# The second norm of an adaLN block: squares written where the normed rows go, and modulated rows of three blocks kept in the place of the decays

## The chip, the cores and the metric

The kernel runs on one core of a Trainium2 chip. The core has a matrix engine (PE; its weight loads are shown apart as PEld), two elementwise engines (DVE, the vector engine, and ACT, the scalar engine), a third one called POOL, and SP, which issues most DMAs. Each engine works through its own list of instructions in order; an instruction waits until the semaphores it names are reached, and everything behind it on that engine waits with it. The metric is the device time of one execution in microseconds (us).

## The reference, cut to what matters

The input is 512 tokens of 1024 numbers. A first norm, attention and a gated linear attention (GLA) give a mixed row per token, which is projected and added to the input; then comes the second norm with its modulation, and a mixer over 16,384 experts (PEER) which finds, per token and head, the best keys:

```python
mixed = jnp.concatenate([att, go], axis=-1) @ w_out[l]
x = x + gate1 * mixed

h2 = rms_norm(x, norm2_w[l]) * (1.0 + scale2) + shift2
x = x + gate2 * peer_ffn(h2, peer_wq[l], peer_subkeys[l], peer_u[l], peer_v[l])
...
q = (h @ wq).reshape(B, S, PEER_HEADS, 2, PEER_QDIM // 2)
sub_scores = jnp.einsum('bshpk,hpnk->bshpn', q, subkeys).astype(jnp.float32)
top_v, top_i = lax.top_k(sub_scores, PEER_TOPK)
...
ub = jnp.take(u, eb, axis=0)
hid = jax.nn.gelu(jnp.einsum('tkd,td->tk', ub, xb), approximate=False) * gb
vb = jnp.take(v, eb, axis=0)
return jnp.einsum('tk,tkd->td', hid, vb)
```

## The kernel before, in words

The tokens are four blocks of 128. The order of the program is: first norm, projections, attention and GLA (about the first 240 us); the output projection (`mixers`, L624) for blocks 0 and 1, then for 2 and 3; the second norm of each block (`second_norm`, L649); the queries of eight heads (`wq_head`, L733), whose scores and top-16 go to DVE; then the gate phase, in which weights of the experts are built for blocks 0 to 2 and products with the first expert table (`u_part`) are done ahead; then the products with the second table. Block 3 is done by gathering the rows of its chosen experts instead (L884, L894).

Every fp32 product is done as three matmuls on a high and a low part (`mm3`, L63 to L66). `hilo` (L55) makes the parts: ACT copies the source to the high part (L59), DVE subtracts (L60).

The second norm of one block n is a chain. ACT squares the row block x1 and sums it along the row (L232, in `norm_stats`), in a tile of the tag `h2_32` that nobody reads; `rstd_of` (L71 to L81) makes the factor in four small DVE and two small ACT instructions; DVE multiplies (L653, the normed rows `xn2`); PE transposes eight squares of 128x128 (L662, `x2t`); DVE and ACT take turns to modulate them into `h32` (L666, L669); ACT rounds the whole block to `h2Th` (L671) and DVE subtracts to get `h2Tl` (L672). For block 3 PE also transposes the modulated rows back (L678), and ACT copies them to `h2n` (L679).

Two pools of one buffer tie blocks together. `xn2` has one buffer (L650). The tag `h2_32` has one buffer too, and both the squares and the modulated rows of a block are in it: the squares of block n+1 (L232) can't be written before `h2Tl` of block n has been read out of it (L672).

`wq_head` for heads 0 and 1 works in halves of 256 tokens: `pq00` and `pq01` (bank tag `ph`) take blocks 0 and 1, are copied to `qha` by ACT (L748), and take blocks 2 and 3. Then come the scores `pss` (L754), from `qha` and the keys `skT`, which SP loads into a part of `scm` (L737).

The order of the work: a scheduler orders the instructions of each engine when the program is built, by its own model of times; only in the gate phase are the orders of DVE and POOL those of the code. Tiles of the pools `frG`, `frT` and `frA` lie on the right side of the on-chip memory. `Eg` (L142, in `frG`) holds the decays of GLA and later its gates; its last use is L545. After the norms, a pool `rt` is opened in the bytes that these pools leave: in it are `qha`, `scm`, and the index tables `iot` (L950) and `ioc` (L953).

Of the kernel before, what the change touches and what calls it, by code (L numbers as in the profile page):

```python
# [7 lines left out]
F32 = mybir.dt.float32  # L8
# [4 lines left out]
AF = mybir.ActivationFunctionType  # L13
# [4 lines left out]
P = 128  # L18
D = 1024
KD = 8  # L20
# [6 lines left out]
NL = 7  # L27
# [14 lines left out]
def peer_block_kernel(ctx: ExitStack, tc: tile.TileContext, a: dict, out: bass.AP):  # L42
    nc = tc.nc
# [27 lines left out]
    def rstd_of(pool, ss, n, w, name):  # L71
        m = pool.tile([P, w], F32, name=name + "m", tag="rsm", bufs=2)
        y = pool.tile([P, w], F32, name=name + "y", tag="rsy", bufs=2)
        t = pool.tile([P, w], F32, name=name + "t", tag="rst", bufs=2)
        nc.vector.tensor_scalar(m, ss, 1.0 / n, EPS, op0=OP.mult, op1=OP.add)
        nc.scalar.activation(y, m, AF.Ln)
        nc.scalar.activation(y, y, AF.Exp, scale=-0.5)
        nc.vector.tensor_tensor(t, y, y, OP.mult)  # L78
        nc.vector.tensor_tensor(t, t, m, OP.mult)
        nc.vector.tensor_scalar(t, t, -0.5, 1.5, op0=OP.mult, op1=OP.add)  # L80
        nc.vector.tensor_tensor(y, y, t, OP.mult)  # L81
        return y
# [34 lines left out]
    def bank(name, tag="m"):  # L117
        return banks["pool"].tile([P, 512], F32, tag=tag, bufs=BUFS[tag], name=name)

    def bank2(name):  # L120
        return psf.tile([P, 2, 512], F32, tag="sc2", bufs=1, name=name)
# [5 lines left out]
    frG = frG_s.enter_context(tc.tile_pool(name="frG", bufs=1, side="right"))  # L127
# [11 lines left out]
            lst.append(frG.tile([P, 2, 2, P], F32, tag="blk", bufs=6, name=f"{nm}{i}"))  # L139
    gv = [frG.tile([P, 512], F32, tag="gv", bufs=NT, name=f"gv{n}") for n in range(NT)]  # L140

    Eg = frG.tile([P, NL + 2, 512], F32, name="Eg")  # L142
    gg = [Eg[:, n, :] for n in range(NT)]
    mixA = [frG.tile([P, 4, P], F32, tag="mixA", bufs=NT + 1, name=f"mixA{n}") for n in range(NT)]
    xn = list(zip(gv, gg))
# [56 lines left out]
    def mod_part(v, pool, tag, bufs, pb=None, dst=None):  # L202
# [18 lines left out]
        else:  # L221
# [3 lines left out]
            nc.vector.tensor_tensor(modT[:, v * 8:v * 8 + 8], pb[:, 0:8], badaT[:, v * 8:v * 8 + 8], OP.add)  # L225
            if v == 4:
                nc.vector.scalar_tensor_tensor(aT[:, 1, :], modT[:, v * 8:v * 8 + 8], 1.0, n2T, op0=OP.add, op1=OP.mult)

    def norm_stats(src, n, pool, tag, bufs, name):
        sq = pool.tile([P, D], F32, tag=tag, bufs=bufs, name=f"sq{name}{n}")  # L230
        ss = pool.tile([P, 1], F32, tag="ss", bufs=2, name=f"ss{name}{n}")
        nc.scalar.activation(sq, src, AF.Square, accum_out=ss)  # L232
        return rstd_of(pool, ss, float(D), 1, f"r{name}{n}")

    for n in range(NT):
        sq = frA.tile([P, D], F32, tag="m4", bufs=2, name=f"sqa{n}")
        ss = frA.tile([P, 2], F32, tag="ss", bufs=2, name=f"ssa{n}")
# [3 lines left out]
        r = rstd_of(frA, ss[:, 0:1], float(D), 1, f"ra{n}")  # L241
# [50 lines left out]
    for half in range(2):  # L292
# [8 lines left out]
        for k in range(4 * half, 4 * half + 4):  # L301
            h32 = frA.tile([P, T], F32, tag="h32", bufs=4, name=f"h32_{k}")
# [311 lines left out]
    frW = frW_s.enter_context(tc.tile_pool(name="frW", bufs=1, side="right", reuse_waits="tile"))  # L614
# [9 lines left out]
    def mixers(n0):  # L624
        pair = (n0, n0 + 1)
        x1s = []
        for n in pair:
            x1s.append(frW.tile([P, D], F32, tag="x1", bufs=4, name=f"x1_{n}"))
            nc.sync.dma_start(x1s[-1], a["x"][n * P:(n + 1) * P, :])
        for q in range(2):  # L630
            qs = slice(q * 512, (q + 1) * 512)
            pw = [bank(f"pw{n}{q}") for n in pair]
            for k4 in range(0, KD, 4):
                wo = raw([P, 4, 512], f"wo{n0}{q}{k4}")
                nc.sync.dma_start(wo, a["w_out"][:, k4:k4 + 4, qs])
                for j in range(0, 4, 2):
                    oh, ol = hilo(wo[:, j:j + 2, :], [P, 2, 512], f"wo{n0}{q}{k4}{j}", nc.vector)
                    for k in (k4 + j, k4 + j + 1):
                        for i, n in enumerate(pair):
                            mm3(pw[i], mixd[n][0][k], mixd[n][1][k], oh[:, k % 2, :], ol[:, k % 2, :], k == 0,  # L640
                                k == KD - 1)
            for i, n in enumerate(pair):
                mg = frW.tile([P, 512], F32, tag="mg", bufs=2, name=f"mg{n}{q}")
                nc.vector.tensor_tensor(mg, pw[i], gate1b[:, qs], OP.mult)
                nc.vector.tensor_tensor(x1s[i][:, qs], x1s[i][:, qs], mg, OP.add)
        for i, n in enumerate(pair):
            second_norm(n, x1s[i])

    def second_norm(n, x1):  # L649
        xn2 = frW.tile([P, D], F32, tag="xn2", bufs=1, name=f"xn2_{n}")  # L650
        nc.sync.dma_start(x1d[n], x1)
        r = norm_stats(x1, n, frW, "h2_32", 1, "b")
        nc.vector.tensor_scalar(xn2, x1, r, None, op0=OP.mult)  # L653
        h32 = frW.tile([P, KD, P], F32, tag="h2_32", bufs=1, name=f"h2_{n}")
        for half in range(2):
            if half == 0 and n % 2 == 0:
                second_norm.two = bank2(f"x2t{n}")
            pt = second_norm.two[:, half] if n % 2 == 0 else bank(f"x2t{n}{half}", ("pt", "po")[half])
            pt = pt.rearrange("p (a b) -> p a b", a=4)
            for i in range(4):  # L660
                k = 4 * half + i
                nc.tensor.transpose(pt[:, i, :], xn2[:, k * P:(k + 1) * P], ident)  # L662
            for i in range(4):
                k = 4 * half + i
                if i % 2:
                    nc.vector.tensor_scalar(h32[:, k, :], pt[:, i, :], aT[:, 1, k:k + 1], modT[:, 24 + k:25 + k],  # L666
                                            op0=OP.mult, op1=OP.add)
                else:
                    nc.scalar.activation(h32[:, k, :], pt[:, i, :], AF.Identity, bias=modT[:, 24 + k:25 + k],  # L669
                                         scale=aT[:, 1, k:k + 1])  # L670
        nc.scalar.activation(h2Th[:, :, n * P:(n + 1) * P], h32, AF.Copy)  # L671
        nc.vector.tensor_tensor(h2Tl[:, :, n * P:(n + 1) * P], h32, h2Th[:, :, n * P:(n + 1) * P], OP.subtract)  # L672
        if n == GB:
            two = bank2("h2n")
            for half in range(2):
                pb = two[:, half]
                for i in range(4):
                    nc.tensor.transpose(pb[:, i * P:(i + 1) * P], h32[:, 4 * half + i, :], ident)  # L678
                nc.scalar.activation(h2n[:, half * 512:(half + 1) * 512], pb, AF.Copy)  # L679
# [465 lines left out]
```

## Time and profile before

| what | us |
|---|---|
| median of three runs | 1573.27 (1570.92 to 1573.38) |
| the profiled execution's own time | 1578.01 |
| its span, first to last instruction | 1576.2 |
| PE busy in the span | 1499.6 (95%) |
| DVE busy | 1254.0 (80%) |
| ACT busy | 689.2 (44%) |
| POOL busy | 410.0 (26%) |
| mean granted TensorE clock | 0.982 |

The profiled execution took 4.74 us more than the median. A busy PE means that a matmul is in flight, not that the array runs at full speed: the clock that was granted is shown apart, where 1.00 is 2.4 GHz and 0.50 is 1.2 GHz. Overlapping matmuls of one engine are each shown with their full duration, so the pace of a row of them is the distance of two starts. In a row of the timeline the bracket gives how long the engine had been idle before the instruction and what ended that. Line numbers are those of the kernel before; the names have lost their numbers, so that `h`, `x2t` or `xn` stand for every block's.

### The profile page before, as it was taken

To read this page: it belongs to the slowest core of one execution; us is meant where nothing else is said; L and a number is where in the kernel's file an instruction comes from. 1 tells how busy PE (TensorE), PEld (TensorE's weight loads), DVE (VectorE), ACT (ScalarE), POOL (GpSimd) and SP (SyncE) were. 2 spreads that over 40 slices of the span, in tenths; PEclk is the share of its full clock that TensorE was granted. 3 is DMA by queue.
4 is the path that set the end of the run, shared out by engine and by line. 5 is a ranking of instruction groups with operands and counts; after the bars stand their busy time and mean duration, and the time that the engine had idled before them with its cause. 6 is when DMAs were issued, how large, how long until landed. Compare 5 with 4: busy or idle time off the path is not lost.

```text
span 1576.2 us, 24415 instructions
## 1 busy us (share of the span) xinstructions
PE 1499.6 (95%) x9379; PEld 1333.6 (85%) x9379; DVE 1254.0 (80%) x2476; ACT 689.2 (44%) x1078; POOL 410.0 (26%) x327
## 2 busy tenths in 40 slices
PE   4998989599999999999899999999999999999997
PEld 3787877598998999899888888888888888888885
DVE  7578567479998988997488788878888888887987
ACT  5545475343354667565233333333333333333343
POOL 1000000044410000004143344343443444334550
PEclk9999899699999999999999999999999999999998
DMA  9254435144344867679988898989998998898893
GB/s 348 84 201 147 150 102 192 60 166 171 129 145 141 266 190 232 203 228 357 400 322 328 329 360 317 350 326 354 345 325 339 340 363 325 325 350 325 294 343 124
DMA packets 154932, 409.67 MB, mean 260 GB/s; under 512 B 10288, under 2 KB 77120, under 8 KB 142400
## 3 DMA queue, kind: packets, MB, share of 16 engines
q1 hardware_dynamic: 108736, 261.30, 46.7%
q0 software_dynamic: 36864, 134.23, 23.0%
q10 hardware_dynamic: 9216, 12.59, 2.2%
q8 instruction: 73, 1.20, 0.3%
q14 instruction: 43, 0.35, 0.1%
HBM read 366.14 MB, written 41.94 MB: 259 GB/s over the span
## 4 chain that ended last, share of the span: by engine, by line
PE 63%; DVE 2%; DMA 2%; ACT 1%; issue 0%; DVEq 0%; ACTq 0%; SPq 0%
PE acc L65 11%; PE acc L64 11%; PE acc L66 11%; PE ph L66 9%; PE ph L64 9%; PE ph L65 9%; PE pg L871 4%; DMA Gd<-gs 1%; DMA gr<-Gd 1%; DVE o L864 0%; ACT gs L873 0%; DVE o L859 0%; DVE oh L816 0%; DVE oh L819 0%; ACT ge L696 0%
## 5 line engine op out<-in xcount | busy, mean ns | idle before, releaser
L884 POOL DMA_INDIRECT gu<-in_u_dram,ix_u x128 | 169.1, 1321 | 531.4 <-DVE o L864 268.3
L894 POOL DMA_INDIRECT gv<-in_vP_dram,ix_v x128 | 168.9, 1320 | 217.8 <-DVE gu L886 187.0
L899 DVE SCALAR_TENSOR_TENSOR gacc<-gv,hg,gacc 128x1024 f32<-128x1024 f32 x127 | 162.6, 1280 | 1.7 <-DMA gv<-in_vP_dram,ix_v 1.5
L886 DVE SCALAR_TENSOR_TENSOR gu<-gu,h2n 128x1024 f32<-128x1024 f32 x128 | 155.9, 1218 | 6.2 <-DMA gu<-in_u_dram,ix_u 6.2
L1025 ACT ACTIVATE Ah<-ge 128x384 fp32r<-128x384 f32 x64 | 33.6, 525 | 157.2 <-PE acc L65 154.5
L1025 ACT ACTIVATE Ah<-gel 128x384 fp32r<-128x384 f32 x64 | 33.6, 525 | 154.4 <-PE acc L65 154.4
L873 ACT ACTIVATE gs<-pg 128x512 f32<-128x512 f32 x96 | 94.0, 1110 | 8.1 <-PE pg L871 8.0
L864 DVE TENSOR_TENSOR o<-o,gp 128x1024 bf16<-128x1024 bf16 x144 | 91.0, 687 | 4.3
L871 PE MATMUL pg<-o,o 128*128 128x128 bf16 x1152 | 77.7, 222 | 4.9 <-DVE o L864 4.9
L871 PEld LDWEIGHTS <-o 128*128 128x128 bf16 x1152 | 68.7, 98 | 13.3 <-issue 7.8
L696 ACT ACTIVATE ge<-ph 128x384 f32<-128x384 f32 x128 | 60.7, 475 | 26.3 <-PE ph L66 26.3
L1026 DVE TENSOR_TENSOR Al<-gel,Ah 128x384 fp32r<-128x384 f32 x64 | 35.5, 555 | 45.2 <-ACT Ah L1025 45.2
L950 POOL IOTA iot<- 128x256 bf16 x1 | 1.5, 1542 | 249.8 <-DVE rb0t L78 249.8
L859 DVE TENSOR_TENSOR o<-iot,t 128x2048 bf16<-128x2048 bf16 x48 | 58.5, 1218 | 4.9 <-ACT t L839 4.9
L1026 DVE TENSOR_TENSOR Al<-ge,Ah 128x384 fp32r<-128x384 f32 x64 | 35.5, 554 | 19.0 <-ACT Ah L1025 16.2
L1021 DVE TENSOR_TENSOR ge<-ge,gr 128x384 f32<-128x384 f32 x64 | 35.4, 552 | 13.3 <-ACT ge L696 13.3
L212 DVE SCALAR_TENSOR_TENSOR macc<-wa,scs,macc 128x1024 f32<-128x1024 f32 x28 | 38.9, 1390 | 5.0 <-DMA wa<-in_w_ada_dram 4.7
L1021 DVE TENSOR_TENSOR gel<-gel,gr 128x384 f32<-128x384 f32 x64 | 32.7, 552 | 0.3 <-DMA gel<-gsp 0.3
L64 PE MATMUL pq<-h2Th,wq_0h 128*128 128x512 f32 (+1 forms) x80 | 29.3, 371 | 3.0 <-ACT h2Th L671 3.0
L65 PE MATMUL pq<-h2Tl,wq_0h 128*128 128x512 f32 (+1 forms) x80 | 29.4, 367 | 0.5 <-DVE h2Tl L672 0.5
L66 PE MATMUL pq<-h2Th,wq_0l 128*128 128x512 f32 (+1 forms) x80 | 28.9, 362 | 0.0
L65 PE MATMUL pq<-h2Tl,wq_1h 128*128 128x512 f32 (+1 forms) x80 | 28.3, 354 | 0.0
(2599 smaller groups left out, 5096.3 us busy)
## 6 DMA issues: line engine op xcount, KB each, us to landing
u<-in_uT_dram SPq DMA_DIRECT2D x64, 1024.0 KB
v<-in_vP_dram SPq DMA_DIRECT2D x64, 1024.0 KB
Gd<-gs SPq DMA_DIRECT2D x24, 1024.0 KB
gr<-Gd SPq DMA_DIRECT2D x16, 1536.0 KB
wa<-in_w_ada_dram SPq DMA_DIRECT2D x20, 1024.0 KB
gsp<-ge ACTq DMA_DIRECT2D x64, 192.0 KB
gel<-gsp SPq DMA_DIRECT2D x32, 384.0 KB
wi<-in_w_in_dram SPq DMA_DIRECT2D x9, 1024.0 KB
```

Source lines behind the costliest of these rows:

```text
L64: nc.tensor.matmul(acc, lh, rh, start=start, stop=False)
L65: nc.tensor.matmul(acc, lh, rl, start=False, stop=False)
L66: nc.tensor.matmul(acc, ll, rh, start=False, stop=stop)
L864: nc.vector.tensor_tensor(o2[:, :, m], o12[:, :, 1], gp3[:, g0:g0 + H, m, None].to_broadcast([P, H, P, 2]), OP.mult)
L871: nc.tensor.matmul(pt[:, i, :], o12[:, g, 0, :, r], o2[:, g, m, :, r], start=(m == 0), stop=(m == 2))
L873: nc.scalar.activation(gs[:, :, t0 + 4 * f:t0 + 4 * f + 4].rearrange("p b a -> p a b"), pt, AF.Copy)
L884: nc.gpsimd.indirect_dma_start(out=ur, out_offset=None, in_=a["u"], in_offset=bass.IndirectOffsetOnAxis(ap=ix_u[:, s:s + 1], axis=0))
L886: nc.vector.scalar_tensor_tensor(ur, ur, 1.0, h2n, op0=OP.mult, op1=OP.mult, accum_out=hid[:, s:s + 1])
L894: nc.gpsimd.indirect_dma_start(out=vr, out_offset=None, in_=a["vP"], in_offset=bass.IndirectOffsetOnAxis(ap=ix_v[:, s:s + 1], axis=0))
L899: nc.vector.scalar_tensor_tensor(gacc, vr, hg[:, s:s + 1], gacc, op0=OP.mult, op1=OP.add)
L1021: nc.vector.tensor_tensor(ge, ge, v_part.g[:, :, c % CG, :], OP.mult)
L1026: nc.vector.tensor_tensor(Al, gef, Ah, OP.subtract)
```

## The change

`norm_stats` is gone. The squares are written into the block's own `xn2` tile, which the normed rows overwrite afterwards; `xn2` gets two buffers in place of one. The modulated rows no longer share a tag with the squares: those of block 0 have a tile of their own (`h2_0`), those of blocks 1 to 3 are three slices of one tile `h2_123`, which takes the place of `Eg` (same tag, one buffer). It can be written once L545 has read the last gate from `Eg`. The number of instructions is the same on every engine. In the new program, the lines from L236 to L647 stand 6 earlier and those from L658 on 3 later; the square is L648 and the store of x1 L646.

```diff
--- before.py
+++ after.py
@@ -139,7 +139,7 @@
             lst.append(frG.tile([P, 2, 2, P], F32, tag="blk", bufs=6, name=f"{nm}{i}"))
     gv = [frG.tile([P, 512], F32, tag="gv", bufs=NT, name=f"gv{n}") for n in range(NT)]
 
-    Eg = frG.tile([P, NL + 2, 512], F32, name="Eg")
+    Eg = frG.tile([P, NL + 2, 512], F32, tag="Eg", bufs=1, name="Eg")
     gg = [Eg[:, n, :] for n in range(NT)]
     mixA = [frG.tile([P, 4, P], F32, tag="mixA", bufs=NT + 1, name=f"mixA{n}") for n in range(NT)]
     xn = list(zip(gv, gg))
@@ -225,12 +225,6 @@
             nc.vector.tensor_tensor(modT[:, v * 8:v * 8 + 8], pb[:, 0:8], badaT[:, v * 8:v * 8 + 8], OP.add)
             if v == 4:
                 nc.vector.scalar_tensor_tensor(aT[:, 1, :], modT[:, v * 8:v * 8 + 8], 1.0, n2T, op0=OP.add, op1=OP.mult)
-
-    def norm_stats(src, n, pool, tag, bufs, name):
-        sq = pool.tile([P, D], F32, tag=tag, bufs=bufs, name=f"sq{name}{n}")
-        ss = pool.tile([P, 1], F32, tag="ss", bufs=2, name=f"ss{name}{n}")
-        nc.scalar.activation(sq, src, AF.Square, accum_out=ss)
-        return rstd_of(pool, ss, float(D), 1, f"r{name}{n}")
 
     for n in range(NT):
         sq = frA.tile([P, D], F32, tag="m4", bufs=2, name=f"sqa{n}")
@@ -647,11 +641,20 @@
             second_norm(n, x1s[i])
 
     def second_norm(n, x1):
-        xn2 = frW.tile([P, D], F32, tag="xn2", bufs=1, name=f"xn2_{n}")
+
+        xn2 = frW.tile([P, D], F32, tag="xn2", bufs=2, name=f"xn2_{n}")
         nc.sync.dma_start(x1d[n], x1)
-        r = norm_stats(x1, n, frW, "h2_32", 1, "b")
+        ss = frW.tile([P, 1], F32, tag="ss", bufs=2, name=f"ssb{n}")
+        nc.scalar.activation(xn2, x1, AF.Square, accum_out=ss)
+        r = rstd_of(frW, ss, float(D), 1, f"rb{n}")
         nc.vector.tensor_scalar(xn2, x1, r, None, op0=OP.mult)
-        h32 = frW.tile([P, KD, P], F32, tag="h2_32", bufs=1, name=f"h2_{n}")
+        if n == 0:
+            h32 = frW.tile([P, KD, P], F32, name="h2_0")
+        else:
+
+            if n == 1:
+                second_norm.h32 = frG.tile([P, NL + 2, 512], F32, tag="Eg", bufs=1, name="h2_123")
+            h32 = second_norm.h32[:, 2 * n - 2:2 * n, :].rearrange("p a (b c) -> p (a b) c", c=P)
         for half in range(2):
             if half == 0 and n % 2 == 0:
                 second_norm.two = bank2(f"x2t{n}")
```

The scheduler moves instructions. On PE, at the end of the mixers (`pw` are their products, `x2t10` and `x2t11` the transposes of block 1, `pq00` the first query product of blocks 0 and 1), before:

```order
L65 MATMUL pw31_2805<-wo2142l_2859,gh3_2487 128x512
L66 MATMUL pw31_2805<-wo2142h_2858,gl3_2488 128x512
L662 MATMUL x2t10_2704<-ident_73,xn2_1_2687 128x128 x4
L662 MATMUL x2t11_2713<-ident_73,xn2_1_2687 128x128 x4
L64 MATMUL pq00_2991<-h2Th_2428,wq0_0h_2982 128x256
L64 MATMUL pq01_2992<-h2Th_2428,wq0_0h_2982 128x256
```

and in the changed kernel:

```order
L66 MATMUL pw21_2802<-wo2142h_2856,gl2_2475 128x512
L64 MATMUL pw31_2803<-wo2142h_2856,gh3_2487 128x512
L65 MATMUL pw31_2803<-wo2142l_2857,gh3_2487 128x512
L66 MATMUL pw31_2803<-wo2142h_2856,gl3_2488 128x512
L64 MATMUL pq00_2985<-h2Th_2428,wq0_0h_2976 128x256
L64 MATMUL pq01_2986<-h2Th_2428,wq0_0h_2976 128x256
```

The eight transposes of block 1 have left this place; they stand some 60 rows further up, among the mixers' matmuls and beside the transposes of block 0, and the query products follow the mixers at once.

On ACT, at the same place in the program (`sqb` are squares, `rb` the factor, `h2_1` the modulated rows of block 1, `wq1_0h` and `uc0h` high parts of weights), before:

```order
L59 ACTIVATE uc0h_3146<-u0_3144 128x1024
L232 ACTIVATE sqb1_2689,ssb1_2690<-x1_1_2497 128x1024
L59 ACTIVATE wq1_0h_3180<-wq1_3178 128x1024
L76 ACTIVATE rb1y_2693<-rb1m_2692 128x1
L77 ACTIVATE rb1y_2693<-rb1y_2693 128x1
L669 ACTIVATE h2_1_2703<-x2t10_2704,modT_83,aT_85 128x128
L669 ACTIVATE h2_1_2703<-x2t11_2713,modT_83,aT_85 128x128
L669 ACTIVATE h2_1_2703<-x2t10_2704,modT_83,aT_85 128x128
L669 ACTIVATE h2_1_2703<-x2t11_2713,modT_83,aT_85 128x128
L671 ACTIVATE h2Th_2428<-h2_1_2703 128x8x128
L232 ACTIVATE sqb2_2882,ssb2_2883<-x1_2_2724 128x1024
```

and in the changed kernel:

```order
L672 ACTIVATE h2_0_2666<-x2t0_2667,modT_83,aT_85 128x128
L59 ACTIVATE uc0h_3140<-u0_3138 128x1024
L674 ACTIVATE h2Th_2428<-h2_0_2666 128x8x128
L59 ACTIVATE wq1_0h_3174<-wq1_3172 128x1024
L648 ACTIVATE xn2_2_2878,ssb2_2880<-x1_2_2722 128x1024
L648 ACTIVATE xn2_3_2912,ssb3_2914<-x1_3_2724 128x1024
L76 ACTIVATE rb2y_2883<-rb2m_2882 128x1
L77 ACTIVATE rb2y_2883<-rb2y_2883 128x1
L76 ACTIVATE rb3y_2917<-rb3m_2916 128x1
L77 ACTIVATE rb3y_2917<-rb3y_2917 128x1
L672 ACTIVATE h2_123_2701<-x2t2_2893,modT_83,aT_85 128x128
```

Block 1's modulation has left this place for the middle of the mixers. The squares of blocks 2 and 3 now stand back to back, and behind them the modulations of both, in turns.

On ACT, at the end of the norms (`h2n` is the copy of block 3's rows, `qha` the queries), before:

```order
L669 ACTIVATE h2_3_2932<-x2t31_2942,modT_83,aT_85 128x128
L679 ACTIVATE h2n_2430<-h2n_2953 128x512
L671 ACTIVATE h2Th_2428<-h2_3_2932 128x8x128
L679 ACTIVATE h2n_2430<-h2n_2953 128x512
L748 ACTIVATE qha_2978<-pq00_2991 128x256
L59 ACTIVATE wq1_1h_3184<-wq1_3178 128x1024
L59 ACTIVATE uc2h_3342<-u0_3144 128x1024
L748 ACTIVATE qha_2978<-pq01_2992 128x256
```

and in the changed kernel:

```order
L672 ACTIVATE h2_123_2701<-x2t2_2893,modT_83,aT_85 128x128
L674 ACTIVATE h2Th_2428<-h2_123_2701 128x8x128
L672 ACTIVATE h2_123_2701<-x2t2_2893,modT_83,aT_85 128x128
L674 ACTIVATE h2Th_2428<-h2_123_2701 128x8x128
L682 ACTIVATE h2n_2430<-h2n_2947 128x512 x2
L751 ACTIVATE qha_2972<-pq00_2985 128x256
L751 ACTIVATE qha_2972<-pq01_2986 128x256
L751 ACTIVATE qha_2972<-pq00_2985 128x256
L59 ACTIVATE wq1_1h_3178<-wq1_3172 128x1024
```

Before, the first halves of `qha` were copied between the modulations of block 2, further up. Now they stand behind `h2n`. The first of them also has a new wait: `rt` reuses the bytes of `h2_123`, so `qha` can't be written before the last `h2Tl` has read that tile. The index tables of L950 and L953 wait for it too, and so do the two `skT` loads, which stand on SP behind two stores of x1 that they preceded before. On PE the second half of `pq00` waits for the copy of its first half.

Further down the lists agree except at eight places in the gate phase, where PE does two matmuls of a next u block (`ph42`, `ph44`, `ph46`, `ph50`, `ph62`, `ph64`), a group of gate matmuls (`pg`) or one transpose earlier; ACT has a copy or a table load moved by a few rows there, and SP two stores.

## Rows read from the trace of the kernel before

**Rows 1.** One page, parts 1 and 4: busy time by engine; the chain's shares
```profile
PE 1499.6 (95%) x9379; PEld 1333.6 (85%) x9379; DVE 1254.0 (80%) x2476; ACT 689.2 (44%) x1078; POOL 410.0 (26%) x327
...
PE 63%; DVE 2%; DMA 2%; ACT 1%; issue 0%; DVEq 0%; ACTq 0%; SPq 0%
```

**Rows 2.** Busy time by stretch, us; then PEclk, DMA share, GB/s
```profile
260.00:280.00 20.00, 15.40 (x69) 11.72 (x66) 15.40 (x23) 10.74 (x16) 0.00 (x0) 1.00 0.48 166
280.00:300.00 20.00, 10.99 (x64) 9.86 (x64) 7.84 (x21) 7.99 (x16) 0.00 (x0) 0.68 0.15 57
300.00:320.00 20.00, 15.65 (x101) 14.73 (x102) 6.18 (x13) 8.48 (x16) 0.48 (x1) 0.72 0.00 1
320.00:450.00 130.00, 130.00 (x731) 118.41 (x730) 118.72 (x780) 47.17 (x67) 61.96 (x46) 1.00 0.44 155
```

**Rows 3.** Waits of PE, 250 to 320 us: total us, times, longest
```profile
PE x2t L662 <- DVE xn L653: 13.1, 2, 7.7
PE pq L64 <- ACT h2Th L671: 3.0, 1, 3.0
```

**Rows 4.** Timeline of ACT: start, us, instruction, [idle before <-releaser]
```profile
285.29 1.06 ACT L671 ACTIVATE h2Th<-h 128x1024 fp32r<-128x1024 f32 x1 [0.48 <-DVE h L666]
287.63 1.06 ACT L232 ACTIVATE sqb<-x 128x1024 f32<-128x1024 f32 x1 [1.29 <-DVE h2Tl L672]
```

**Rows 5.** Timeline of DVE, the tail of the second norm
```profile
272.95 1.22 DVE L672 TENSOR_TENSOR h2Tl<-h,h2Th 128x1024 fp32r<-128x1024 f32 x1
...
279.42 0.69 DVE L645 TENSOR_TENSOR x<-x,mg 128x512 f32<-128x512 f32 x1
...
290.24 0.76 DVE L653 TENSOR_SCALAR xn<-x,rb2y 128x1024 f32<-128x1024 f32 x1
```

**Rows 6.** Timeline of PE, from the mixers' last matmul to the scores
```profile
275.60 0.40 PE L66 MATMUL pw<-wo2142h,gl 128*128 128x512 f32 x1
281.40 1.97 PE L662 MATMUL x2t<-ident,xn 128*128 128x128 f32 x8 [5.40 <-DVE xn L653]
286.39 0.79 PE L64 MATMUL pq<-h2Th,wq_0h 128*128 128x256 f32 x2 [3.02 <-ACT h2Th L671]
...
288.25 0.41 PE L64 MATMUL pq<-h2Th,wq_0h 128*128 128x256 f32 x1
288.46 0.41 PE L65 MATMUL pq<-h2Tl,wq_0h 128*128 128x256 f32 x1
...
291.16 0.28 PE L64 MATMUL pq<-h2Th,wq_1h 128*128 128x256 f32 x1
291.28 0.28 PE L65 MATMUL pq<-h2Tl,wq_1h 128*128 128x256 f32 x1
...
318.30 1.05 PE L754 MATMUL pss<-scm,qha 128*128 128x128 f32 x8
```

**Rows 7.** Busy time by microsecond, with the granted clock (PEclk)
```profile
280.00:281.00 1.00, 0.00 (x0) 0.00 (x0) 0.90 (x5) 0.00 (x0) 0.00 (x0) 0.77 0.96 367
281.00:282.00 1.00, 0.60 (x3) 0.60 (x4) 0.34 (x1) 0.00 (x0) 0.00 (x0) 0.50 1.01 406
...
291.00:292.00 1.00, 1.00 (x11) 1.00 (x10) 0.00 (x0) 0.00 (x0) 0.00 (x0) 1.00 0.00 0
```

**Rows 8.** Groups of instructions, 276 to 318.3 us: busy, mean ns, idle before
```profile
L669 ACT ACTIVATE h<-x2t,modT,aT 128x128 f32<-128x128 f32 x12 | 5.3, 456 | 11.9 <-PE x2t L662 10.7 <-DVE h L666 1.0
...
L666 DVE TENSOR_SCALAR h<-x2t,aT,modT 128x128 f32<-128x128 f32 x12 | 4.8, 410 | 10.3 <-ACT h L669 10.3
```

**Rows 9.** Waits of PE after 320 us
```profile
PE ph L64 <- ACT ge L696: 6.3, 4, 3.6
PE pg L871 <- DVE o L864: 4.9, 8, 1.7
```

**Rows 10.** One weight tile of the gate phase: duration ns, first and last start
```profile
L64 PE MATMUL ph<-h2Th,uc42h x8: 334/334/423, 509.2 to 512.9; 128*128 128x384 f32 x8
...
L59 ACT ACTIVATE uc42h<-u x1: 1062/1062/1062, 483.8 to 483.8; 128x1024 fp32r<-128x1024 f32 x1
```

## The prediction

> **What bounds the kernel now.** I read the page's shares first, then busy time by stretch, then the waits of the engine that the first two point to, and last the timelines of the place where it waits. PE is busy in 95% of the span and holds 63% of the chain that ended last, with no other engine above 2% [rows 1]. So a microsecond in which PE stands still for another engine's work is worth about a microsecond at the end, as long as PE isn't held again later for the same reason. The stretches show where it stands still: of 260 to 320 us it is busy in 15.40, 10.99 and 15.65 us out of 20 each, and there the clock falls to 0.68 and 0.72; from 320 to 450 us it is busy all the time at 1.00 [rows 2]. DMA carries nearly nothing in 280 to 320 us (a share of 0.15 and 0.00), so no transfer is behind it.
>
> The waits name it: 13.1 us in two places for the normed rows `xn`, the longer 7.7 us, and 3.0 us for `h2Th` [rows 3]. That is the second norm's chain, and ACT's timeline shows why blocks don't overlap: the square of block 2 began 1.29 us after ACT was free, released by the subtraction that makes `h2Tl` [rows 4], because squares and modulated rows share one buffer. x1 of block 2 was long there: the last x1 row of the mixers ended at 279.42 + 0.69 = 280.1 us [rows 5], and that square began at 287.63.
>
> The price of the stretch is read on PE. The mixers' last matmul ends at 275.60 + 0.40 = 276.0 us, and the scores `pss` begin at 318.30 [rows 6]: 42.3 us. In them PE has 120 query matmuls of 256 columns (by the code, 96 of head 0 in two halves and 24 of head 1) and 32 transposes (three blocks, and the `h2n` ones). The pace of the query matmuls is 288.46 - 288.25 = 0.21 us at half clock and 291.28 - 291.16 = 0.12 us at full clock [rows 6]. Eight transposes took 1.97 us at half clock [rows 6], so about 1.0 at full clock (an estimate by the ratio of the levels). All of it at full clock and without a wait is 14.4 + 4.0 = 18.4 us, so that no reordering of this stretch alone can bring more than 42.3 - 18.4 = 23.9 us; and since block 1's eight transposes leave it, 24.9.
>
> **The change part by part.** Counts of instructions don't change; what changes is what may start when.
>
> *Block 1 into the mixers.* Its square goes to its own tile and needs `h2Tl` of block 0 no more, so its chain runs beside block 0's. It brings into 256 to 276 us one square and one `h2Th` (1.06 each [rows 4]), four modulations on ACT (4 x 0.456) and four on DVE (4 x 0.41) [rows 8], a multiplication of 0.76 and a subtraction of 1.22 on DVE [rows 5]: some 4 us on each engine. ACT has room (10.74 of 20 busy), DVE too (15.40) [rows 2]. On PE, eight transposes of 1.0 us together come between the mixers' matmuls; PE is idle for 4.6 us in 260 to 280, 4.0 of them after 276.0, so 0.6 us can be hidden and the mixers end at 276.0 + 0.4 = 276.4. If the cover is gone, the whole 1.0 us counts, 0.6 more.
>
> *First half of the query products.* Before, it began at 286.39 [rows 6], after block 1. Now it waits for `h2Tl` of block 0, which ended at 272.95 + 1.22 = 274.2 [rows 5] and now has the low parts of `wq0` and of u0 and block 1's own `h2Tl` among the work ahead of it, two to three subtractions of 1.22: about 277.1. PE idles 0.7 us there, against 5.4 + 3.0 before. 48 matmuls at 0.12 take 5.8 us: 282.9. This removes the wait of 5.4 us in front of block 1's transposes [rows 6], and the 3.0 us behind them.
>
> *Blocks 2 and 3 together.* x1 of block 3 is ready at 280.1 as before, since the mixers end at the same time. From the start of a square to the start of the normed rows it took 290.24 - 287.63 = 2.6 us; both normed rows of 0.76 [rows 4, 5] follow, the factor of block 3 ahead of block 2's rows: 280.1 + 2.6 + 2 x 0.76 = 284.3. PE has its query products until 282.9 and waits some 0.7 us for block 2's first transposes and less for block 3's. Then sixteen modulations: eight on ACT (0.456) and eight on DVE (0.41). In one block they go one after another, DVE idle 10.3 us over twelve of them because each waits for ACT's [rows 8]; in two blocks one engine can be in either. I count eight ACT modulations (3.7 us), `h2Th` of block 3 (1.06), with some 2 us of turns not overlapped, from 283.6 to 290.5, then `h2Th` of block 2 to 291.6 and its `h2Tl` to 292.8. The 24 query products of head 1 and the transposes for `h2n` lie inside these. Before, these were two chains in a row, the second begun when the first's `h2Tl` was done [rows 4].
>
> *The new wait.* `qha`, the first thing written into the bytes of `h2_123`, comes behind that `h2Tl`, and ACT needs some 0.9 us for it and what stands before: PE starts the second half at 293.7, and `pss` after 48 matmuls of 0.12 at 299.5. Behind the `qha` copy on ACT wait the next weight splits, which PE needs only after the second half. The `skT` loads (two of 128 KB) go out at 293 now instead of at 276. The trace shows no landing time for them alone. They have 6.5 us until `pss`, with DMA idle: at the 367 to 406 GB/s that it moved near 281 us [rows 7], 0.26 MB is under 1 us (an estimate); I cost them at nothing and take 6.5 us as what has to pass before they cost.
>
> *The clock.* By these steps PE never stands still for more than about 1 us, but from 283 to 293.7 it is busy for only about half of the time. Before, it stood still for 5.4 us after 276.0, and the clock fell from 1.00 to 0.50 within 280 to 282 us; it was at 1.00 again at 291 us, inside the dense query products that ran from 288.25 on [rows 6, 7]. If it stays at 1.00, `pss` is at 299.5 and the gain 318.3 - 299.5 = 18.8 us. If it falls and the 48 last matmuls all go at 0.21, that is 4.5 us more: 304.0 and a gain of 14.3. No row shows the clock in a half-busy stretch, so both ends stay in the range. I take the fall with a return as in before, inside the dense second half: the 2.8 us from 288.25 to 291 at 0.21 in place of 0.12 cost 2.8 x 0.09 / 0.21 = 1.2 us, and 1.0 us for what of the transposes and head 1's products at half clock isn't hidden (all of the 24 is 24 x 0.09 = 2.2). The gain is 18.8 - 1.2 - 1.0 = 16.6, taken as 16.5 us, the middle of the two ends.
>
> **The sum.** The profiled execution has 1578.01 us, 1.8 of it outside the span of 1576.2. After `pss` PE runs without a gap, and the lists behind it agree but for eight places, so the gain is carried to the end: 1561.5 for an execution like the profiled one. It is 4.74 us above the median, and the gain is a difference inside one execution, so for the median 1573.27 - 16.5 = **1556.8 us**.
>
> **Rivals.**
> (B) *Half clock to the scores.* PE's half-busy stretch drops the clock to 0.50 and the second half doesn't raise it in time: 14.3 us of gain, 1559.0. For it: in 280 to 320 us the mean was 0.68 and 0.72 [rows 2]. Against: the clock came back inside the dense products of the first half, at 291 [rows 6, 7], and the second half has as many. The Trainium skill ("TensorE: Matmul & The Clock Gate", Part 1) says that the throttled level is the default and that activity releases it, which would make the fall in the light stretch the rule. The trace agrees for a PE that stands still, 0.50 at 281 us [rows 7], and is silent on a half-busy one.
>
> (C) *The overlap is only partial.* The modulations of blocks 2 and 3 still go one after another, because each engine's list alternates blocks and a wait for one holds the other. Then the last `h2Tl` is at about 297 instead of 292.8, and the light stretch longer: `pss` at 299.5 + 4.2 + 4.5 = 308.2, gain 10.1, 1563.2. For it: the 10.3 us of turns on DVE [rows 8]. Against: a lone block took from 281.4 (its transposes) to 287.6 (the `h2Tl` that released the square) [rows 4, 6], 6.2 us at half clock, and even two of these in a row from 283.6 end at 296.0.
>
> (D) *Slower: the eight places of the gate phase.* There PE's list has a u matmul earlier than before, and it needs a bank that ACT's `ge` has to empty. PE's in-order list then stands. `ph` waited for `ge` 6.3 us in four places before, 3.6 at the longest [rows 9]. At 3.6 in each of eight places it costs 28.8 us, against a gain of 16.5: 1573.3 + 12.3 = 1585.6. It decides from 16.5 / 8 = 2.06 us a place. Against it: the other operand stands far ahead (`uc42h` is done at 484.9, used at 509.2 [rows 10]), and only one or two of a part's 24 matmuls move.
>
> (E) *Given back later.* The query stage gains, and the gate phase, with DVE busy in 118.72 of 130 us from 320 on [rows 2], takes it back, since its selections can't be done sooner. Then PE shows new waits for `o` in place of the 4.9 us [rows 9] and the time stays within 0.2%, 1571 to 1573. Against: the selections start with the scores, which come sooner by the same amount, and PE had no gap in these 130 us.
>
> (F) *More than forecast.* Clock at 1.00 throughout and the 2 us of turns gone: 18.8 + 2.0 = 20.8, 1552.5.
>
> **How the numbers follow.** The forecast's own range is 1554.5 (18.8 us, the clock at 1.00) to 1558. Chances: forecast 0.46, (B) 0.21, (C) 0.17, (F) 0.09, (E) 0.04, (D) 0.03. The range for 8 in 10 holds (F) and what of it goes a microsecond further, (B), and (C) with two more: 1551 to 1565. A difference of 0.2% (3.1 us) is about what a measurement of this kernel can tell from no change. Faster: 0.46 + 0.21 + 0.17 + 0.09 = 0.93; within 0.2%: 0.04; slower: 0.03.
>
> **What would show it.** In the profile after: no square waiting for an `h2Tl`, and the squares of 2 and 3 back to back near 279 to 281 us; `pq` starting within 1.5 us of the mixers' end; PE's wait for `xn` down from 13.1 to under 2 us; last `h2Tl` near 293 and `pss` between 299 and 305; the clock in 283 to 299 decides between the forecast and (B). Wrong would be a wait of `pss` for the `skT` load, `pss` after 308, or new waits of `ph` or `pg` past 320 us larger than the 6.3 and 4.9 us of before.

## The result, and the profile after

The changed kernel takes 1556.59 us (median of six, 1554.75 to 1562.43), the kernel before 1573.33 (median of six, 1570.92 to 1576.38). The ratio is 0.990 with a 95% interval of 0.9879 to 0.992: 12.6 to 19.0 us faster. The forecast was 1556.8. Two later measurements of the same kernel gave 0.9893 (0.9874 to 0.9912) and 0.9904 (0.9888 to 0.992).

The profiled execution took 1555.13 us, its span 1553.4: 22.9 us under the profiled execution of before, so more than the medians say. Where that comes from is seen by cutting both spans at the mixers' last matmul and at the first scores. In the changed kernel, PE's timeline from one to the other (start, us, instruction, [idle before <-releaser]) is:

```profile
271.42 0.40 PE L66 MATMUL pw<-wo2142h,gl 128*128 128x512 f32 x1
271.65 0.40 PE L64 MATMUL pq<-h2Th,wq_0h 128*128 128x256 f32 x2
273.22 0.39 PE L65 MATMUL pq<-h2Tl,wq_0h 128*128 128x256 f32 x1 [1.17 <-DVE h2Tl L675]
...
279.24 0.66 PE L665 MATMUL x2t<-ident,xn 128*128 128x128 f32 x4 [0.25 <-DVE xn L650]
280.10 1.09 PE L665 MATMUL x2t<-ident,xn 128*128 128x128 f32 x8 [0.20 <-DVE xn L650]
282.10 0.66 PE L665 MATMUL x2t<-ident,xn 128*128 128x128 f32 x4 [0.91 <-DVE h L669]
...
287.64 0.66 PE L681 MATMUL h2n<-ident,h 128*128 128x128 f32 x4 [0.92 <-ACT h2n L682]
289.26 0.39 PE L64 MATMUL pq<-h2Th,wq_0h 128*128 128x256 f32 x1 [0.96 <-ACT qha L751]
...
295.12 1.05 PE L757 MATMUL pss<-scm,qha 128*128 128x128 f32 x8
```

The mixers end at 271.42 + 0.40 = 271.82 us, against 276.0 [rows 6]; the scores `pss` start at 295.12, against 318.30. What lies behind them took 1553.4 - 295.1 = 1258.3 us, against 1576.2 - 318.3 = 1257.9. So the 22.8 us between the spans are 4.2 ahead of the stretch, 42.3 - 23.3 = 19.0 in it, and -0.4 behind it. The brackets show what is left: PE stands still for 0.2 to 1.2 us at a time, where before it stood for 5.40, 3.02 and 7.7 us [rows 3, 6].

One row of the busy time by stretch, cut at these two points, shows it in one line (length; busy us of PE, PEld, DVE, ACT, POOL; PEclk, DMA share, GB/s). Before:

```profile
276.00:318.30 42.30, 24.95 (x152) 22.89 (x153) 17.07 (x40) 16.31 (x32) 0.00 (x0) 0.72 0.16 56
```

After:

```profile
271.82:295.12 23.30, 18.71 (x145) 16.92 (x144) 12.52 (x29) 12.28 (x25) 1.87 (x2) 1.00 0.20 76
```

PE's idle time went from 42.30 - 24.95 = 17.35 us to 23.30 - 18.71 = 4.59: 12.8 of the 19.0 us. Its busy time went from 24.95 to 18.71 at a mean clock of 0.72 and then 1.00: 6.2 us, of which 1.97 is the row of block 1's transposes at half clock [rows 6], which moved into the mixers (eight at 1.00 take 1.09 us above); the other 4.3 us go with the clock. PE's waits of the stretch, which answer to [rows 3] (us in total, times, longest):

```profile
PE pq L65 <- DVE h2Tl L675: 1.2, 1, 1.2
PE pq L64 <- ACT qha L751: 1.0, 1, 1.0
PE h2n L681 <- ACT h2n L682: 0.9, 1, 0.9
PE x2t L665 <- DVE h L669: 0.9, 1, 0.9
PE x2t L665 <- DVE xn L650: 0.4, 2, 0.2
```

The 13.1 us for `xn` are 0.4. On ACT, the squares of blocks 2 and 3 (L648) follow x1 and no longer an `h2Tl`, in contrast to [rows 4]:

```profile
274.40 1.06 ACT L648 ACTIVATE xn<-x 128x1024 f32<-128x1024 f32 x1 [1.49 <-DVE x L639]
...
276.14 1.06 ACT L648 ACTIVATE xn<-x 128x1024 f32<-128x1024 f32 x1 [0.58 <-DVE x L639]
...
279.94 0.46 ACT L672 ACTIVATE h<-x2t,modT,aT 128x128 f32<-128x128 f32 x1 [2.00 <-PE x2t L665]
280.80 2.46 ACT L672 ACTIVATE h<-x2t,modT,aT 128x128 f32<-128x128 f32 x6 [0.40 <-PE x2t L665]
...
288.83 0.65 ACT L751 ACTIVATE qha<-pq 128x256 f32<-128x256 f32 x2
```

The six modulations from 280.80 took 2.46 us in one row, 0.41 each without a gap: with two blocks in turn ACT hardly waits for DVE's. On DVE, the `h2Tl` of block 0, for which the query products wait, and the last one, which frees the place of `h2_123`:

```profile
271.95 1.22 DVE L675 TENSOR_TENSOR h2Tl<-h,h2Th 128x1024 fp32r<-128x1024 f32 x1
...
287.13 1.23 DVE L675 TENSOR_TENSOR h2Tl<-h,h2Th 128x1024 fp32r<-128x1024 f32 x1 [1.12 <-ACT h2Th L674]
```

The first query copy on ACT starts at 288.83, behind that last `h2Tl` (288.36) and behind the second `h2n` copy, and it has no idle time before it: the bytes of `h2_123` were free before ACT got there. PE waits 0.96 us for the copy. This comes from the copy's place in ACT's list, and it is the most that the new wait costs PE at this point.

In the gate phase the eight places that the order moved cost little. PE's waits from 305 us on, which answer to [rows 9]:

```profile
PE pg L874 <- DVE o L867: 5.3, 10, 1.7
PE ph L64 <- ACT ge L699: 3.7, 3, 2.8
```

They are 9.0 us together, against 11.2 before; the other profiles of the changed kernel have 11.2 and 9.4, the second one of the kernel before 10.6. The waits for `ge` are 3.7 to 5.8 us, against 6.3 and 5.6. Those for `o` are 5.3 to 5.5 us in ten places, against 4.9 and 5.0 in eight.

### The profile page after: what moved, and what is told of

Its sections match the earlier page's. It is cut to its first block, busy times and chain, and to the rows that moved or that the text cites. A ratio compares the mean times of both kernels' runs of the same rounds, so it can differ in the third digit from the quotient of the medians.

```text
span 1553.4 us, 24408 instructions
## 1 busy us (share of the span) xinstructions
PE 1493.2 (96%) x9379; PEld 1328.2 (86%) x9379; DVE 1251.8 (81%) x2476; ACT 688.8 (44%) x1078; POOL 412.9 (27%) x327
## 4 chain that ended last, share of the span: by engine, by line
PE 63%; DVE 3%; DMA 2%; ACT 1%; issue 1%; DVEq 0%; ACTq 0%; SPq 0%
PE acc L65 11%; PE acc L64 11%; PE acc L66 11%; PE ph L66 8%; PE ph L64 8%; PE ph L65 8%; PE pg L874 4%; DMA Gd<-gs 1%; DMA gr<-Gd 1%; DVE o L867 1%; ACT gs L876 0%; DVE o L862 0%; DVE oh L819 0%; DVE oh L822 0%; DVE oh L817 0%
## 5 line engine op out<-in xcount | busy, mean ns | idle before, releaser
L953 POOL IOTA iot<- 128x256 bf16 x1 | 1.5, 1541 | 282.8 <-DVE h2Tl L675 282.8
L66 PE MATMUL pq<-h2Th,wq_1l 128*128 128x512 f32 (+1 forms) x80 | 28.2, 352 | 0.0
```

The costliest lines, as they stand in the source:

```text
L66: nc.tensor.matmul(acc, ll, rh, start=False, stop=stop)
```

## The experiments

In this section the stretch is always from the end of the mixers' last matmul to the start of the first scores.

**The kernel before and the changed kernel again.** No edit. Open was whether the 4.2 us ahead of the stretch belong to the change.

> The kernel before unaltered, for a second profile. Theory 2: the stretch from the mixers' last matmul to the first scores takes 42.3 us again within 1, and the mixers' end lies between 271 and 277 us by the clock of 140 to 180 us. Rival (the change shortens the first 276 us): the mixers' end is at 275 to 277 us again.

> The changed kernel unaltered, for a second profile and a closer ratio. Theory 2 (the 4.3 us by which its mixers began and ended sooner than in the profile of the kernel before come from a clock dip at 140 to 180 us that differs from execution to execution, in a part where the two programs are alike): the mixers' end lies somewhere between 271 and 277 us with the granted clock of 140 to 180 us deciding it, the stretch to the first scores takes 23.4 us again within 0.5, and the ratio is 0.987 to 0.991. Rival (the change itself makes the first 276 us shorter): the mixers' end is again at 271 to 272 us whatever the clock shows, and the ratio 0.985 to 0.987.

> The changed kernel unaltered, on the same chip as the run with separate banks, and as a third profile. Theory 2 (the clock at 160 to 180 us and in the light stretch differs from execution to execution): mixers' end at 271 to 277 us by the clock of 140 to 180 us, the stretch 23.3 us if its clock stays at 1.00 and 24.7 if it falls once, from pss to the end 1258 us within 1. Ratio 0.988 to 0.991.

The busy time by stretch holds the answer, by the clock (third column from the right) in 160 to 180 us. The kernel before, first and second profile:

```profile
160.00:180.00 20.00, 20.00 (x307) 14.88 (x306) 12.37 (x25) 8.20 (x28) 0.00 (x0) 0.74 0.57 196
```

```profile
160.00:180.00 20.00, 20.00 (x348) 16.42 (x348) 16.71 (x48) 11.91 (x43) 0.00 (x0) 1.00 0.57 208
```

And the slice directly behind it in the second profile, 180 to 200 us:

```profile
180.00:200.00 20.00, 20.00 (x137) 16.16 (x138) 7.87 (x22) 8.90 (x22) 0.00 (x0) 0.91 0.17 53
```

The changed kernel, first and second profile:

```profile
160.00:180.00 20.00, 20.00 (x346) 16.29 (x343) 16.34 (x49) 12.73 (x45) 0.00 (x0) 1.00 0.51 183
```

```profile
160.00:180.00 20.00, 20.00 (x267) 14.58 (x269) 12.41 (x23) 8.10 (x27) 0.00 (x0) 0.74 0.63 219
```

Each kernel has one execution with 0.74 and one with 1.00, and the mixers end accordingly: at 276.0 and 272.6 us before, at 271.8 and 277.2 us in the changed kernel (the third profile of it: 1.00 and 271.9).

Theory 2 holds for most of it: a long fall of the clock at 160 to 180 us came in one of two executions before and in one of three after, and the pair of first profiles happened to be one of each. The others aren't free of a fall, they have a shorter one further on: 0.91 in 180 to 200 us (the second profile of before) or in 200 to 220 us (the first and third of the changed kernel). By these rows the long fall costs 20 x (0.26 - 0.09) = 3.4 us more than the short one, which is the distance of the two profiles of before. The changed kernel's lie 5.4 us apart; some 2 us of that aren't explained by these slices.

The rival, that the change shortens the start, falls by the 277.2, which is later than both mixers' ends of before. What the change does there can be read inside the mixers: from the first product with `wo2000h` to the mixers' end it is 276.00 - 250.94 = 25.06 and 25.01 us in the two profiles before, and 25.19, 25.21 and 25.19 in the three after. So block 1's transposes cost the mixers 0.2 us, and the rest of the differences lies ahead of the second norm.

The stretch of the kernel before is 42.17 us in the second profile; that of the changed kernel 24.73 and 23.29 in the second and third:

```profile
272.64:314.81 42.17, 24.81 (x154) 22.75 (x154) 17.08 (x40) 16.30 (x32) 0.00 (x0) 0.76 0.15 56
```

```profile
277.17:301.90 24.73, 20.17 (x145) 18.38 (x144) 12.46 (x29) 12.28 (x25) 1.87 (x2) 0.93 0.19 72
```

```profile
271.87:295.16 23.29, 18.70 (x144) 16.90 (x144) 12.51 (x29) 12.27 (x25) 1.87 (x2) 1.00 0.20 77
```

The ratios are those given above.

The 24.73 us lie outside the 23.4 within 0.5 that was expected of the second profile, and they are no scatter of the chain: the waits are the same five to a tenth of a microsecond. In this execution the clock fell in the stretch:

```profile
292.00:293.00 1.00, 0.08 (x2) 0.03 (x1) 0.53 (x1) 0.92 (x2) 0.00 (x0) 1.00 0.00 0
293.00:294.00 1.00, 0.63 (x4) 0.39 (x4) 0.70 (x1) 0.33 (x1) 0.16 (x1) 1.00 0.00 0
294.00:295.00 1.00, 0.41 (x3) 0.41 (x4) 0.00 (x0) 0.82 (x3) 1.00 (x1) 1.00 0.10 28
295.00:296.00 1.00, 1.00 (x7) 1.00 (x7) 0.00 (x0) 0.00 (x0) 0.71 (x2) 0.55 0.68 212
296.00:297.00 1.00, 1.00 (x7) 1.00 (x6) 0.00 (x0) 0.00 (x0) 0.00 (x0) 0.50 0.07 23
...
298.00:299.00 1.00, 1.00 (x8) 1.00 (x8) 0.00 (x0) 0.00 (x0) 0.00 (x0) 0.74 0.00 0
299.00:300.00 1.00, 1.00 (x10) 1.00 (x10) 0.00 (x0) 0.38 (x1) 0.00 (x0) 1.00 0.00 0
```

PE was busy for 0.08, 0.63 and 0.41 us of three microseconds, the clock went to 0.50 behind that, and came back at 298 to 299 us inside the second half's products. It cost 24.73 - 23.30 = 1.4 us. In the other two executions the same work, with the same gaps, kept 1.00 throughout.

**Only the squares.** The modulated rows keep one buffer for all blocks:

```diff
-        if n == 0:
-            h32 = frW.tile([P, KD, P], F32, name="h2_0")
...
+        h32 = frW.tile([P, KD, P], F32, tag="h2_32", bufs=1, name=f"h2_{n}")
```

> Only the squares move: they go into the block's own xn2 with two buffers, and the modulated rows keep one buffer (tag h2_32) for all four blocks. Theory 1 (the shared buffer made squares of the next block wait, and that wait was the chain): squares of blocks 2 and 3 start together near the mixers' end, and only the modulations stay one block after another. From the durations of the changed kernel's trace, the last h2Tl comes some 3 to 4 us later than there, and the stretch from the mixers' last matmul to the first scores (42.3 us before, 23.4 in the changed kernel) takes 26 to 28 us: time 14 to 16 us under the kernel before, ratio 0.990 to 0.991. Rival (only both halves of the change together free the blocks): the modulations wait as the squares did, the stretch takes 37 us or more, and the time is within 5 us of the kernel before, ratio 0.997 to 1.000. On the clock: if a half-busy PE keeps 1.00, as in the changed kernel's trace, the stretch shows 1.00 wherever PE's gaps stay near 1 us, and a drop where PE stands still for several us.

It took 1567.05 us (seven runs), ratio 0.9958 (0.9945 to 0.9971), some 7 us faster, and its stretch 34.55 us. Neither theory 1 (26 to 28) nor the rival (37 or more) had that. PE's waits say why:

```profile
PE pq L64 <- ACT h2Th L668: 6.5, 1, 6.5
PE h2n L675 <- ACT h L666: 4.8, 1, 4.8
```

No wait for `xn` is left, so the squares did stand in the chain. But the first query products multiply blocks 0 and 1 in one go of 256 columns. Block 1's modulated rows can't be written before block 0's `h2Tl`, and so its `h2Th` comes 6.5 us after the mixers. Block 3's rows wait for block 2's in the same way, and PE stands 4.8 us before it can transpose them back for `h2n`. Both stops also cost the clock: the mean of the stretch is 0.80.

```profile
272.84:307.39 34.55, 22.77 (x146) 21.42 (x145) 15.02 (x34) 14.54 (x28) 0.00 (x0) 0.80 0.18 69
```

**Only the place of the modulated rows.** The squares have a tile of their own, `xn2` one buffer:

```diff
-        xn2 = frW.tile([P, D], F32, tag="xn2", bufs=2, name=f"xn2_{n}")
+        xn2 = frW.tile([P, D], F32, tag="xn2", bufs=1, name=f"xn2_{n}")
...
-        nc.scalar.activation(xn2, x1, AF.Square, accum_out=ss)
+        sq = frW.tile([P, D], F32, tag="sq2", bufs=1, name=f"sqb{n}")
+        nc.scalar.activation(sq, x1, AF.Square, accum_out=ss)
```

> Only the place of the modulated rows moves: block 0 has its own tile, blocks 1 to 3 lie in the place of Eg; the squares go to a tile of their own with one buffer and xn2 keeps one buffer. Theory 1: squares no longer wait for h2Tl, but the normed rows of block 3 wait until PE has transposed block 2's. The stretch from the mixers' last matmul to the first scores takes 25 to 28 us, the time is 14 to 17 us under the kernel before, ratio 0.989 to 0.991: either half alone gives most of it, since either one takes the squares out of the modulated rows' buffer. Rival (both halves needed): 37 us or more in the stretch, ratio 0.997 to 1.000. Second rival (the new wait of the queries' copy for the bytes of h2_123 costs): with the same wait here and not in the run with the squares alone, this one is the slower of the two by 2 us or more.

It took 1565.07 us (five runs), ratio 0.9946 (0.9928 to 0.9964), some 8.5 us faster; the stretch is 32.14 us. Again between the two, and for a reason of the same kind:

```profile
PE pq L64 <- ACT h2Th L675: 5.3, 1, 5.3
...
PE x2t L666 <- DVE xn L651: 0.8, 1, 0.8
```

```profile
273.94:306.08 32.14, 22.43 (x145) 20.89 (x145) 13.94 (x32) 14.03 (x28) 1.87 (x2) 0.84 0.18 70
```

Block 1's normed rows can't be written before PE has transposed all of block 0; its transposes now stand near the end of the mixers (270.33 us in this trace), and the query products wait 5.3 us for its `h2Th`. The second rival, that the wait for the bytes of `h2_123` makes this run the slower of the two, falls: it has that wait (0.96 us for `qha`, as in the changed kernel) and isn't slower.

So each half of the change takes away a part of its own. In the stretch they bring 7.6 and 10.0 us against the second profile of before, and both together 17.4 to 18.9: the two gains add up. What only both together remove is most of the stop in front of the first query products: 5.4 + 3.0 us before [rows 6], 6.5 and 5.3 us in the single halves, 1.2 in the changed kernel.

**The clock by itself.** The kernel before, with transposes of the identity in PE's waits, whose results nobody reads:

```diff
+                if n == 2 and q == 1:
+                    for _ in range(36):
+                        nc.tensor.transpose(pw[0][:, 0:P], ident, ident)
...
+        if n == 1:
+            for _ in range(10):
+                nc.tensor.transpose(pt[:, 0, :], ident, ident)
+        if n == 2:
+            for _ in range(24):
+                nc.tensor.transpose(pt[:, 0, :], ident, ident)
```

> The kernel before with 70 extra transposes of the identity on PE, whose results nobody reads: 36 behind the mixers' last matmul, 10 in front of the first query products, 24 behind block 2's transposes. They lie inside PE's waits (5.4, 3.0 and 7.7 us) and take none of the chain's waits away. Theory 3 (of the 42.3 us of the stretch, 24.95 are busy time that would be some 18.5 at full clock, so a part of what the change gained is the clock that fell while PE stood still): with PE kept busy the clock stays at 1.00 through block 1's transposes and the first query products, these end 2 to 3 us sooner, block 2's chain begins sooner, and the stretch takes 36 to 39 us: 3 to 6 us gained with all the shared buffers of before, ratio 0.996 to 0.998. Rival (the waits alone count, the clock costs nothing because the chain of the norms sets the end): the stretch stays at 41.5 to 43 us, ratio 0.999 to 1.001.

```profile
274.20 4.15 PE L648 MATMUL pw<-ident 128*128 128x128 f32 x36 [1.12 <-DVE rb1m L75]
278.50 1.09 PE L665 MATMUL x2t<-ident,xn 128*128 128x128 f32 x8 [0.15 <-DVE xn L656]
281.53 1.31 PE L676 MATMUL x2t<-ident 128*128 128x128 f32 x10 [1.93 <-DVE h L669]
...
294.49 4.51 PE L679 MATMUL x2t<-ident 128*128 128x128 f32 x24 [1.93 <-DVE h L669]
300.25 1.09 PE L665 MATMUL x2t<-ident,xn 128*128 128x128 f32 x8 [1.25 <-DVE xn L656]
...
312.07 1.05 PE L763 MATMUL pss<-scm,qha 128*128 128x128 f32 x8
```

```profile
273.07:312.07 39.00, 29.52 (x223) 27.35 (x223) 17.21 (x40) 16.35 (x32) 0.00 (x0) 0.96 0.17 61
```

Block 1's eight transposes took 1.09 us in place of the 1.97 of [rows 6], the first query products ran at full clock, and the mean clock is 0.96 in place of 0.72 and 0.76. It fell once, for less than 4 us, and only dead transposes ran in that time:

```profile
295.00:296.00 1.00, 1.00 (x7) 1.00 (x6) 0.44 (x1) 0.53 (x1) 0.00 (x0) 0.50 0.00 0
...
298.00:299.00 1.00, 1.00 (x9) 0.76 (x7) 0.45 (x3) 0.41 (x2) 0.00 (x0) 0.94 0.00 0
```

The stretch takes 39.0 us: 3.2 less than the second profile of before, the smallest gain that theory 3 allowed. In the time it is not resolved: 1572.1 us, ratio 0.9998 (0.9987 to 1.0009), which is at most 2 us faster. So theory 3 just holds in the stretch and misses its ratio of 0.996 to 0.998, and the rival misses the stretch and has the ratio. The trace of one execution shows about 3 us for the clock alone, and the times don't confirm as much. It is the smaller part either way: with a full clock and the waits of before, the chain of the norms still holds PE up, and 39.0 - 23.3 = 15.7 us of the stretch remain for the waits (1.1 of them are block 1's transposes, which are still in the stretch here).

**The rest of the waits.** The changed kernel, with block 2's transposes and `h2n` in single banks, and the `h2n` copies on DVE:

```diff
-            if half == 0 and n % 2 == 0:
+            if half == 0 and n == 0:
                 second_norm.two = bank2(f"x2t{n}")
-            pt = second_norm.two[:, half] if n % 2 == 0 else bank(f"x2t{n}{half}", ("pt", "po")[half])
+            pt = second_norm.two[:, half] if n == 0 else bank(f"x2t{n}{half}", ("pt", "po")[half] if n % 2 else "m")
...
-                pb = two[:, half]
+                pb = bank(f"h2n{half}", "m")
...
-                nc.scalar.activation(h2n[:, half * 512:(half + 1) * 512], pb, AF.Copy)
+                nc.vector.tensor_copy(h2n[:, half * 512:(half + 1) * 512], pb)
```

> The changed kernel with the rest of its waits taken on: block 2's transposes go to two separate banks of the tag m in place of one tile of two banks, so that the second half doesn't wait for the modulation of the first; the h2n transposes too, and their two copies go from ACT to DVE, so that ACT gets to the queries' copy sooner. Theory: PE stands still 4.6 us in the stretch of the changed kernel; the waits of 0.9 (x2t for h), 0.9 (h2n for its copy) and part of 1.0 (qha) go, the stretch is 21 to 22.5 us against 23.3 to 24.7, and the time 1.5 to 2.5 us under the changed kernel's, 1554 to 1556, ratio to the kernel before 0.9875 to 0.989. Rival (ACT and DVE are the bound there, sixteen modulations, two h2Th and two h2Tl in a row, whatever PE does): the stretch stays at 23 to 24.7 and the time at the changed kernel's.

```profile
279.40 1.97 PE L665 MATMUL x2t<-ident,xn 128*128 128x128 f32 x16 [0.27 <-DVE xn L650]
282.28 0.44 PE L680 MATMUL h2n<-ident,h 128*128 128x128 f32 x2 [0.91 <-DVE h L669]
...
287.79 0.39 PE L64 MATMUL pq<-h2Th,wq_0h 128*128 128x256 f32 x1 [1.16 <-ACT qha L750]
...
293.64 0.61 PE L756 MATMUL pss<-scm,qha 128*128 128x128 f32 x4
```

All sixteen transposes of blocks 2 and 3 are now in one row, and the scores start 21.66 us after the mixers (271.98 to 293.64), against 23.30: 1.6 us less. Of the three waits that were to go, that of the transposes for `h` is gone. `h2n` still waits, now 0.91 us for a modulation in place of 0.92 for its copy, and the wait for `qha` grew from 0.96 to 1.16 us. The `h2n` copies on DVE stand ahead of the last `h2Tl`, and ACT, which has nothing left to copy, stands idle for 2.29 us until that `h2Tl` frees the bytes:

```profile
287.35 0.66 ACT L750 ACTIVATE qha<-pq 128x256 f32<-128x256 f32 x2 [2.29 <-DVE h2Tl L675]
```

So in this variant the new wait is what holds the query products.

The time is 1554.61 us (five runs), ratio 0.9885 (0.9869 to 0.9901), against 1557.48 and 0.9904 (0.9888 to 0.992) for the changed kernel on the same chip. The stretch fell as expected, and the rival, that it stays at 23 to 24.7, falls; the intervals of the two ratios overlap, so that the times alone don't tell the two apart. It is faster than the kernel before beyond doubt.

## Why the prediction was right

By its own steps:

- *Block 1 into the mixers* and *the first half of the query products*: right. The mixers were to get 0.4 us longer and got 0.2. Forecast was an idle time of 0.7 us ahead of the query products; the first two, which need only `h2Th`, followed the mixers at once, and then PE waited 1.17 us for block 0's `h2Tl`. The experiments add that this needs both halves of the change.
- *Blocks 2 and 3 together*: right. The last `h2Tl` was forecast 292.8 - 276.0 = 16.8 us after the mixers' end of before, and ended 288.36 - 271.82 = 16.5 us after the mixers' end of its own trace. Rival (C), turns one after another, is refuted by the six modulations of 0.41 us in one row.
- *The new wait*: right in place and size. From the last `h2Tl` to the second half of the query products 0.9 us were forecast, and it took 289.26 - 288.36 = 0.90. But what PE waits for in that time is ACT's list, with `h2n` ahead of the copy, and no longer the bytes. The `skT` loads never show as a releaser of `pss`.
- *The clock*: the step with the wrong size. The forecast took a fall with a return for granted, at 1.2 + 1.0 us. Two of three profiles kept 1.00 and a third fell for 1.4 us. Forecast were 18.8 us of gain in the stretch with the clock at 1.00, and 16.6 with the fall; measured were 19.0 and, against the same 42.3, 17.6. So the sum without the clock's term was right to 0.2 us, and the 16.5 that was taken was 1.1 to 2.5 us too low for the stretch. The low end has a small slip: 48 matmuls at 0.09 us more are 4.3 us and not 4.5, so that rival (B) would have gained 14.5 us; the forecast hardly moves by it. Rival (B), half clock to the scores, didn't come. Its rule from the Trainium skill ("TensorE: Matmul & The Clock Gate", Part 1: throttled by default, released by activity) is not refuted, but it didn't decide here. The same section of the Trainium skill says that the moment at which the clock rises at a kernel's start varies from run to run, because the chip's activity monitor runs freely and doesn't start anew with the kernel. The traces here show a variation too, in the middle of a kernel: 0 and 1.4 us for the same instructions; that it has the same reason isn't shown.
- *Carried to the end*: right but for a microsecond. From the first scores to the end it is 1257.9 and 1257.5 us before, 1258.3 (twice) and 1258.7 after: a loss of 0.4 to 1.2 us, whose cause stays open. Of the signs named for being wrong, one was crossed by a little: the waits for `o` are 5.3 to 5.5 us against 4.9. That is far from the 12 us of rival (D), or from the whole gain that rival (E) takes back.

That the median hit to 0.2 us is in part luck. By the stretch the gain is 17.4 to 19.0 us, less about 0.7 behind it and 0.2 in the mixers; the medians say 16.7 us with an interval of 12.6 to 19.0, and executions of one kernel differ by up to 7.7 us. The clock's term, taken at 2.2 us where 0 to 1.4 were measured, and the small losses outside the stretch balance in part; the rest lies within the scatter.

One sentence of the prediction treats the profile's distance of 4.74 us from the median as a constant. Most of it goes back to the long fall of the clock at 160 to 180 us, which this execution had and the second profile of the same kernel, at 1574.11 us, had not. The forecast didn't suffer, since it added the gain to the median.

## What to carry to other kernels

When a stage shows the fast engine waiting for a chain of small steps, look for the tile that two steps of different blocks share, scratch data first of all; and try the shared tiles together, since each of them alone can hold the first consumer that needs two blocks at once. Before a difference of two profiles is explained, cut both spans at the same instructions and compare the parts: here a fifth of the difference lay ahead of the stretch, where the change itself is worth 0.2 us. Price the waits by the chain and the clock apart: filling the waits with dead work raised the clock and brought little, taking them away brought nearly all.

## What the runs showed of the hardware that was not expected

- The same instructions with the same gaps ran at 1.00 throughout in two executions and fell to 0.50 for about 3 us in a third (0.08, 0.63 and 0.41 us busy in the three microseconds ahead of it). So a half-busy stretch cost 0, 0 and 1.4 us in three executions.
- With PE fully busy in the records of 160 to 180 us, the clock there was 0.74 in two of the five profiles of the two kernels and 1.00 in the other three and in all four variants. Those seven had a shorter fall instead, 0.91 in one of the next two slices of 20 us. Between the two profiles of the kernel before this moved everything behind it by 3.4 us.
- Dead work is enough to bring the clock back: in the run with the extra transposes it fell to 0.50 by 295 us and was back at 298 to 299 us (0.94, then 1.00), inside the row of 24 transposes of the identity.
